# The value part of each chunk's right-hand side, computed in runs ahead of a chunked scan

## The chip, the cores and the metric

The kernel runs on one core of a Trainium2 chip. The metric is the device time of one execution, in microseconds (us). The kernel before took 1484.86, 1486.97 and 1489.13 us in three runs; the median is 1486.97.

## The reference

One step of a hybrid decoder layer, for 512 prompt tokens and 8 samples of 8 tokens (576 columns in all): a half-step SwiGLU network, three mixers side by side that are merged by gates (an RWKV-7 recurrence, a causal convolution, cross-attention into a memory), and a second half-step SwiGLU network. The change touches the recurrence alone. For each of eight heads it keeps a 64 x 64 state and goes token by token:

```python
def step(s, inp):
    r_t, w_t, k_t, v_t, kk_t, kka_t = inp
    sa = jnp.einsum('bhij,bhj->bhi', s, -kk_t)
    s = (s * w_t[:, :, None, :] + sa[..., None] * kka_t[:, :, None, :]
         + v_t[..., None] * k_t[:, :, None, :])
    return s, jnp.einsum('bhij,bhj->bhi', s, r_t)
```

The prompt starts from a zero state, each sample from its own. Outputs are the tokens' results and the states at the end.

## The kernel before

**The whole.** The first network, the mixers, the merge and the second network follow each other. All large products take their operands split into a high and a low part (helper `split`: a cast on ScalarE, L96, and a subtraction on VectorE, L97) and make three products of 128 x 128 weights with 288 columns (`mm3k`, L110). In the mixers such products are also the **filler** that runs beside the recurrence: projections, gates and the parts of the merge that are ready. A table, `PLAN`, writes down in which order the pieces are emitted; the framework's scheduler then interleaves them with a model of its own. Each engine works through its own queue strictly in the order that came out.

**The recurrence in chunks.** Two heads share the 128 partitions, so there are four head pairs j, each prepared (`prep`), partly inverted (`inverse`, on VectorE, then `joined`, two sets of sixteen 32 x 32 products, L987 and L995) and run by a **chain** (`chain`, L877). A chain has nine chunks of 64 tokens: eight of the prompt, one after the other, and a ninth (index 8) with the 64 tokens of the eight samples. `prep` makes, by L872 and a masking L874, the table `gr` of products inside each chunk.

The chain first transposes keys into `kbt` (L890) and values into rows 0 to 63 of `vu` (L894), four chunks to a PSUM bank, and copies them out on ScalarE (L895 for the values). Rows 64 to 127 of `vu` will hold the *solutions*, the vectors `sa` of each token in the chunk. They solve a triangular system; its right-hand side has a value part and a state part. Per prompt chunk c:

1. The value part: for each of the two heads a product of `gr` rows 0 to 63 with the values (L1003).
2. The state part: `ra` times the state before, added in the same PSUM bank (L1006).
3. ScalarE copies the sum to the tile `xs` (L1008); PE multiplies it by the inverse, head by head (L1010); ScalarE copies the solutions into `vu` (L1012).
4. `kbt` times the whole `vu` gives what the chunk adds to the state (L1021). ScalarE scales the old state (L1026) and VectorE forms the new one (L1030; L1033 in the first chunk), in a ring of three `st` tiles.
5. The outputs: L1036 for both heads and L1038 with the old state, copied out on ScalarE (L1039).

After the eight chunks follows `sample_chunk` (L1045): the same with eight states `ms` at once, so that L1006 and the outputs L1058 (eight columns each) are issued eight times; L1067 makes the additions to the states, L1070 and L1071 apply them on VectorE, and L1072 stores them. Then come centering (L904), sums (L138) and the gate (L128). The chain takes its PSUM banks from a pool of three (tag "c"); prep has two ("g"), the filler three ("p").

In the profile's names `st`, `xs`, `vu`, `kbt`, `gr`, `ra` and `ms` are the tiles above, `x`, `wh` and `wl` activations and split weights of the filler, `oc0h` and the like the split operands of merge products, `cst` the constants (identity among them), `lt`, `tt` and `pr` tiles of the inverse (its steps on VectorE are L965, L967 and L969), and `cc` the convolution's sum (L655, L656).

Of the kernel before, what the change touches and what calls it, by code (L numbers as in the profile page):

```python
# [6 lines left out]
F32 = mybir.dt.float32  # L7
F32R = mybir.dt.float32r
AF = mybir.ActivationFunctionType
ALU = mybir.AluOpType  # L10
# [6 lines left out]
NB = 8  # L17
# [33 lines left out]
class _Builder:  # L51
# [825 lines left out]
    def chain(self, j):  # L877
        V, A, T = self.V, self.A, self.T
        con, par = self.con, self.par
        ident = con("ident")  # L880
        b3 = self.b3
        gr, kb, v, ra, gc, bv = self.made[j]

        kbt = b3.tile([128, 9, 128], F32, name="kbt")
        vu = b3.tile([128, 9, 128], F32, name="vu")
        for c in range(0, 9, 4):
            n = min(4, 9 - c)
            ps = self.bank("c")
            for i in range(n):
                T.transpose(ps[:, i * 128:(i + 1) * 128], kb[:, c + i].rearrange("p a t -> p (a t)"), ident)  # L890
            A.copy(kbt[:, c:c + n, :], ps[:, :n * 128].rearrange("p (i t) -> p i t", t=128))
            ps = self.bank("c")
            for i in range(n):
                T.transpose(ps[:64, i * 128:(i + 1) * 128], v[:, (c + i) * 64:(c + i + 1) * 64], ident)  # L894
            A.copy(vu[:64, c:c + n, :], ps[:64, :n * 128].rearrange("p (i t) -> p i t", t=128))  # L895
        self.chunks(j, gr, kbt, vu, ra, gc)
        self.sample_chunk(j, gr, kbt, vu, ra, gc)


        sq, rs = (b3.tile([128, 640], F32, name="u2", bufs=2)[:, :N] for _ in range(2))  # L900
        for c0, c1 in ((0, 5), (5, 9)):
            c = slice(64 * c0, 64 * c1)
            p = self.bank("c")[:, :64 * (c1 - c0)]
# [91 lines left out]
                T.matmul(ps[64:96, h, c, :], zz[:, h, c, :32], gr[96:128, h, c, 96:128], start=True, stop=True)  # L995
        A.copy(gr[64:96, :, :8, 96:128], ps[64:96])

    def solve(self, c, gr, vu, inter):

        T = self.T  # L1000
        ps = self.bank("c")
        for h in range(2):
            T.matmul(ps[64:, 64 * h:64 * h + 64], gr[:64, h, c, 64:], vu[:64, c, 64 * h:64 * h + 64],  # L1003
                     start=h == 0 or not inter, stop=not inter)
        for i, (l, r) in enumerate(inter):
            T.matmul(ps[64:, :128], l, r, start=False, stop=i == len(inter) - 1)  # L1006
        xs = self.b3.tile([128, 128], F32, name="xs")
        self.A.copy(xs[64:], ps[64:, :128])  # L1008
        for h in range(2):
            T.matmul(ps[64:, 128 + 64 * h:192 + 64 * h], gr[64:, h, c, 64:], xs[64:, 64 * h:64 * h + 64],  # L1010
                     start=True, stop=True)
        self.A.copy(vu[64:, c, :], ps[64:, 128:256])  # L1012
        return ps

    def chunks(self, j, gr, kbt, vu, ra, gc):

        V, A, T = self.V, self.A, self.T
        m = None
        for c in range(8):
            ps = self.solve(c, gr, vu, [(ra[:, c, 1, :], m)] if c else [])  # L1020
            T.matmul(ps[:, 256:384], kbt[:, c, :], vu[:, c, :], start=True, stop=True)  # L1021
            self.st = self.st[1:] + self.st[:1]
            mn = self.st[0]
            if c:
                mg = self.b3.tile([128, 128], F32, name="mg", bufs=2)
                A.activation(mg, m, AF.Copy, scale=gc[:, c:c + 1])  # L1026
            for h in range(2):
                s = slice(64 * h, 64 * h + 64)
                if c:
                    V.scalar_tensor_tensor(mn[s, s], ps[s, 256 + 64 * h:320 + 64 * h], gc[s, c:c + 1], mg[s, s],  # L1030
                                           ALU.mult, ALU.add)
                else:
                    V.tensor_scalar(mn[s, s], ps[s, 256 + 64 * h:320 + 64 * h], gc[s, c:c + 1], None, ALU.mult)  # L1033
            for h in range(2):
                s = slice(64 * h, 64 * h + 64)
                T.matmul(ps[s, 384:448], vu[:, c, s], gr[:, h, c, :64], start=True, stop=c == 0)  # L1036
            if c:
                T.matmul(ps[:, 384:448], m, ra[:, c, 0, :], start=False, stop=True)  # L1038
            A.copy(ra[:, c, 0, :], ps[:, 384:448])  # L1039
            m = mn  # L1040
        for h in range(2):
            s = slice(64 * h, 64 * h + 64)
            self.store(self.a["wso"][j, s], m[s, s])

    def sample_chunk(self, j, gr, kbt, vu, ra, gc):  # L1045
        V, A, T = self.V, self.A, self.T
        b3 = self.b3
        ms, ax = self.ms, self.ax
# [5 lines left out]
        for h in range(2):  # L1054
            s = slice(64 * h, 64 * h + 64)
            T.matmul(ps[s, 384:448], vu[:, 8, s], gr[:, h, 8, :64], start=True, stop=False)
        for b in range(NB):
            T.matmul(ps[:, 384 + 8 * b:392 + 8 * b], ms[:, b, :], ra[:, 8, 0, 8 * b:8 * b + 8], start=False,  # L1058
                     stop=b == NB - 1)
        A.copy(ra[:, 8, 0, :], ps[:, 384:448])  # L1060
# [169 lines left out]
```

## Time and profile before

| | us |
|---|---|
| runs | 1484.86, 1486.97, 1489.13 |
| the profiled execution | 1487.49 |
| its span, first to last instruction | 1485.7 |
| PE (TensorE) busy | 1460.2 |
| weight loads busy (PEld) | 1378.1 |
| DVE (VectorE) busy | 1027.4 |
| ACT (ScalarE) busy | 675.5 |
| the four chains and what runs beside them | about 590 to 1000 |

The mean granted clock of TensorE was 0.982. In the rows, "c<-vu,gr" means that a tile of pool "c" was written from `vu` and `gr`; "64*64 64x64 ... x4" is the loaded weight, the columns streamed, and how many records the row holds. In a row of waits the three numbers are the sum in us, how many times, and the longest. Times in timelines count from the start of the span, and the second number is the duration. A number with "<-" in brackets is the engine's idle time just before, and what ended it.

### The profile page before, as it was taken

Reading aid. Unit: us, or ns where it says so; the run is one execution under the profiler, and the core shown is the slowest. Engines: PE = TensorE matmul, PEld = TensorE weight load, DVE = VectorE, ACT = ScalarE, POOL = GpSimd, SP = SyncE. Lnnn points to the kernel's source line nnn. Section 1 sums busy time; section 2 is a strip of 40 time slices with the busy share of each in tenths; the row PEclk is TensorE's granted clock in tenths of the full one; section 3 lists DMA queues with packets and bytes.
Section 4 is the critical chain, followed back from the end, with each engine's and each line's share of the span. In section 5 each row is a group of like instructions: output and inputs, shape, how many; then the busy total and the mean of one; then the engine's idle time right before and its main releaser. Section 6 shows DMA issues by size and latency. Waiting matters only on the chain.

```text
span 1485.7 us, 27013 instructions
## 1 busy us (share of the span) xinstructions
PE 1460.2 (98%) x10778; PEld 1378.1 (93%) x10778; DVE 1027.4 (69%) x2053; ACT 675.5 (45%) x1370; POOL 4.5 (0%) x21
## 2 busy tenths in 40 slices
PE   8999999999999999999999999999999999999997
PEld 8999999999998799888889888789999999999997
DVE  7976777777784579778466456357578767777775
ACT  6443344443577535435446542444354434444342
POOL 0000000000010000000000000000000000000000
PEclk9999999999999999999899999999999999999998
DMA  6222222232632243133123134255222322322221
GB/s 209 72 84 87 86 86 86 86 98 95 205 101 86 66 132 91 46 98 96 60 65 97 55 100 126 92 177 175 100 72 72 100 73 85 102 95 89 86 86 64
DMA packets 95033, 144.04 MB, mean 97 GB/s; under 512 B 43628, under 2 KB 53228, under 8 KB 94908
## 3 DMA queue, kind: packets, MB, share of 16 engines
q1 hardware_dynamic: 94332, 141.74, 30.9%
q8 instruction: 84, 1.38, 0.4%
q10 hardware_dynamic: 576, 0.59, 0.1%
q14 instruction: 41, 0.34, 0.1%
HBM read 126.07 MB, written 16.23 MB: 96 GB/s over the span
## 4 chain that ended last, share of the span: by engine, by line
PE 92%; DVE 4%; ACT 2%; DMA 1%; issue 1%; SPq 0%; DVEq 0%; ACTq 0%
PE p L110 51%; PE p L369 26%; PE g L872 1%; PE c L1006 1%; PE c L1010 1%; PE c L1003 1%; DVE pr L965 1%; PE g L128 1%; PE c L128 1%; PE c L1038 1%; PE c L1036 1%; DMA w<-win 1%; PE p L148 1%; PE c L1021 1%; PE c L1058 1%
## 5 line engine op out<-in xcount | busy, mean ns | idle before, releaser
L110 PE MATMUL p<-x,wh 128*128 128x288 f32 x3136 | 655.4, 300 | 1.1 <-ACT kv L541 0.7
L110 PEld LDWEIGHTS p<-x,wh 128*128 128x128 f32 x3136 | 507.1, 188 | 15.2 <-issue 7.9
L110 PE MATMUL p<-x,wl 128*128 128x288 f32 x1568 | 469.7, 300 | 1.5 <-DVE wl L97 1.5
L96 ACT CAST wh<-w 128x512 fp32r<-128x512 f32 (+1 forms) x353 | 209.5, 600 | 257.2 <-PE p L110 111.9
L97 DVE TENSOR_TENSOR wl<-w,wh 128x512 fp32r<-128x512 f32 (+1 forms) x353 | 231.9, 662 | 109.2 <-ACT wh L96 102.2
L110 PEld LDWEIGHTS p<-x,wl 128*128 128x128 f32 x1568 | 295.2, 188 | 7.0 <-issue 3.1
L369 PE MATMUL p<-t,wh 128*128 128x288 f32 x1088 | 224.2, 298 | 0.0
L369 PEld LDWEIGHTS p<-t,wh 128*128 128x128 f32 x1088 | 173.8, 188 | 6.4 <-DVE t L380 6.2
L369 PE MATMUL p<-b,wh 128*128 128x288 f32 x816 | 169.7, 295 | 0.0
L369 PE MATMUL p<-t,wl 128*128 128x288 f32 x544 | 160.5, 295 | 0.0
L96 ACT CAST wh<-p 128x512 fp32r<-128x512 f32 x136 | 84.5, 621 | 155.9 <-PE p L110 117.7
L369 PEld LDWEIGHTS p<-b,wh 128*128 128x128 f32 x816 | 132.6, 188 | 0.0
L97 DVE TENSOR_TENSOR wl<-p,wh 128x512 fp32r<-128x512 f32 x136 | 93.5, 688 | 50.4 <-ACT wh L96 47.8
L369 PE MATMUL p<-b,wl 128*128 128x288 f32 x408 | 120.3, 295 | 0.0
L369 PEld LDWEIGHTS p<-t,wl 128*128 128x128 f32 x544 | 102.4, 188 | 0.0
L369 PEld LDWEIGHTS p<-b,wl 128*128 128x128 f32 x408 | 76.8, 188 | 0.0
L446 DVE SCALAR_TENSOR_TENSOR x<-p,x 128x288 f32<-128x288 f32 x128 | 57.7, 451 | 20.3 <-PE p L110 20.3
L96 ACT CAST x<-t 128x576 fp32r<-128x576 f32 (+1 forms) x60 | 36.5, 610 | 45.6 <-DVE t L450 42.3
L1030 DVE SCALAR_TENSOR_TENSOR st<-c,gc,mg 64x64 f32<-64x64 f32 x56 | 15.9, 283 | 53.3 <-PE c L1021 52.5
L359 DVE TENSOR_TENSOR p<-w 128x512 f32<-128x512 f32 x68 | 46.7, 686 | 3.2 <-DMA w<-wu 2.7
L359 DVE TENSOR_TENSOR p<-p,w 128x512 f32<-128x512 f32 x68 | 46.3, 681 | 0.1
L110 PE MATMUL p<-x,t 128*128 128x288 f32 x264 | 38.5, 306 | 5.5 <-ACT t L96 5.5
(345 smaller groups left out, 1987.8 us busy)
## 6 DMA issues: line engine op xcount, KB each, us to landing
w<-wu SPq DMA_DIRECT2D x85, 512.0 KB
w<-win SPq DMA_DIRECT2D x44, 512.0 KB
w<-wd SPq DMA_DIRECT2D x64, 256.0 KB
w<-wd SPq DMA_DIRECT2D x16, 384.0 KB
d_mb<-gate SPq DMA_DIRECT2D x16, 288.0 KB
w<-wo SPq DMA_DIRECT2D x8, 512.0 KB
x<-x SPq DMA_DIRECT2D x8, 288.0 KB
d_x<-x SPq DMA_DIRECT2D x16, 144.0 KB
```

The source lines that it names most:

```text
L96: self.A.copy(hi, x)
L97: self.V.tensor_tensor(lo, x, hi.bitcast(F32), ALU.subtract)
L110: self.T.matmul(p, l, x[r][:, c], start=k == 0 and i == 0, stop=k == n - 1 and i == 2)
L128: self.T.matmul(p, l, r[:, c], start=i == 0, stop=i == len(ops) - 1)
L148: self.T.matmul(p[:, o + f - d.start:o + 128 - d.start], r[f:, i], self.con("ident")[f:, f:], start=True, stop=True)
L359: V.tensor_tensor(s, u, v, ALU.add)
L369: self.T.matmul(p, hl[l][:, c], xs[k][b][:, o], start=first and k == 0 and q == 0, stop=k == 3 and q == 2, skip_group_check=True)
L446: V.scalar_tensor_tensor(x[m][:, c], p, 0.5, x[m][:, c], ALU.mult, ALU.add)
L872: T.matmul(ps[:, i * 128:(i + 1) * 128], kb[o, c + i].rearrange("p a t -> p (a t)"), ra[o, c + i].rearrange("p a t -> p (a t)"), start=Tru ...
L965: V.tensor_tensor(pr, tt[:, :n, :e].unsqueeze(2).broadcast_to([np_, n, m, e]), l3[:, t:e, :e].unsqueeze(1).broadcast_to([np_, n, m, e]), A ...
L1003: T.matmul(ps[64:, 64 * h:64 * h + 64], gr[:64, h, c, 64:], vu[:64, c, 64 * h:64 * h + 64], start=h == 0 or not inter, stop=not inter)
L1030: V.scalar_tensor_tensor(mn[s, s], ps[s, 256 + 64 * h:320 + 64 * h], gc[s, c:c + 1], mg[s, s], ALU.mult, ALU.add)
```

## The change

The values of all nine chunks are transposed first. The value parts of the right-hand sides are then computed in runs over four chunks and both heads: eight products into one PSUM bank, a second eight, and two for the ninth chunk. ScalarE copies each run into the rows of `vu` that will later hold the solutions. Between the runs stand the transposes of the keys. In a chunk the state product now fills a bank alone; VectorE adds it to what lies in `vu`, in place; the inverse is applied from there, and the solutions overwrite it. The tile `xs` is gone. Chunk 0 has no state part and takes the rows as they are.

The samples' chunk is cut in four pieces. Right-hand side: ahead of chunk 0. Solution: after chunk 0's. Outputs: ahead of chunk 1. The states: after chunk 1's solution.

```diff
         vu = b3.tile([128, 9, 128], F32, name="vu")
-        for c in range(0, 9, 4):
-            n = min(4, 9 - c)
+        groups = [(c, min(4, 9 - c)) for c in range(0, 9, 4)]
+        by = lambda ps, n: ps[:, :n * 128].rearrange("p (i t) -> p i t", t=128)
+        for c, n in groups:
+            ps = self.bank("c")
+            for i in range(n):
+                T.transpose(ps[:64, i * 128:(i + 1) * 128], v[:, (c + i) * 64:(c + i + 1) * 64], ident)
+            A.copy(vu[:64, c:c + n, :], by(ps[:64], n))
+        for c, n in groups:
+
+            ps = self.bank("c")
+            for i in range(n):
+                for h in range(2):
+                    o = slice(64 * h, 64 * h + 64)
+                    T.matmul(by(ps[64:], n)[:, i, o], gr[:64, h, c + i, 64:], vu[:64, c + i, o], start=True, stop=True)
+            A.copy(vu[64:, c:c + n, :], by(ps[64:], n))
             ps = self.bank("c")
             for i in range(n):
                 T.transpose(ps[:, i * 128:(i + 1) * 128], kb[:, c + i].rearrange("p a t -> p (a t)"), ident)
...
-        self.chunks(j, gr, kbt, vu, ra, gc)
-        self.sample_chunk(j, gr, kbt, vu, ra, gc)
+        sample = self.sample_chunk(j, gr, kbt, vu, ra, gc)
+        self.chunks(j, gr, kbt, vu, ra, gc, lambda: next(sample, None))
...
-    def solve(self, c, gr, vu, inter):
-
-        T = self.T
-        ps = self.bank("c")
+    def solve(self, c, gr, vu, ps):
+
         for h in range(2):
-            T.matmul(ps[64:, 64 * h:64 * h + 64], gr[:64, h, c, 64:], vu[:64, c, 64 * h:64 * h + 64],
-                     start=h == 0 or not inter, stop=not inter)
-        for i, (l, r) in enumerate(inter):
-            T.matmul(ps[64:, :128], l, r, start=False, stop=i == len(inter) - 1)
-        xs = self.b3.tile([128, 128], F32, name="xs")
-        self.A.copy(xs[64:], ps[64:, :128])
+            self.T.matmul(ps[64:, 128 + 64 * h:192 + 64 * h], gr[64:, h, c, 64:], vu[64:, c, 64 * h:64 * h + 64],
+                          start=True, stop=True)
+        self.A.copy(vu[64:, c, :], ps[64:, 128:256])
...
         for c in range(8):
-            ps = self.solve(c, gr, vu, [(ra[:, c, 1, :], m)] if c else [])
+            if c < 2:
+                beside()
+            ps = self.bank("c")
+            if c:
+                T.matmul(ps[64:, :128], ra[:, c, 1, :], m, start=True, stop=True)
+                V.tensor_tensor(vu[64:, c, :], ps[64:, :128], vu[64:, c, :], ALU.add)
+            self.solve(c, gr, vu, ps)
+            if c < 2:
+                beside()
             T.matmul(ps[:, 256:384], kbt[:, c, :], vu[:, c, :], start=True, stop=True)
...
-        ps = self.solve(8, gr, vu, [(ax[:, b, :], ms[:, b, :]) for b in range(NB)])
...
+        ps = self.bank("c")
         for b in range(NB):
...
+            T.matmul(ps[64:, :128], ax[:, b, :], ms[:, b, :], start=b == 0, stop=b == NB - 1)
+        V.tensor_tensor(vu[64:, 8, :], ps[64:, :128], vu[64:, 8, :], ALU.add)
+        yield
+        self.solve(8, gr, vu, ps)
+        yield
+        self.outputs(8, gr, vu, ra, ps, [(slice(8 * b, 8 * b + 8), ms[:, b, :]) for b in range(NB)])
+        yield
```

`outputs` is a new function with the products of step 5 and their copy. New line numbers: value transposes L891, runs L899 and their copy L900, key transposes L903, inverse applied L1010, outputs L1018 and L1020, state product L1033, the add L1034, addition to the state L1038, new state L1047 and L1050, samples' right-hand side L1068, their states L1079, L1081, L1084 and L1085, centering L913; join L996 and L1004.

The order of instructions shows the move at three places. A chunk step of the second chain on PE, before:

```order
L1036 MATMUL c<-gr,vu 64x64 x2
L1038 MATMUL c<-ra,st_5290 128x64
L1006 MATMUL c<-st_5291,ra 64x128
L110 MATMUL p<-x_4933,wh 128x288
L110 MATMUL p<-x_4932,wl 128x288
L110 MATMUL p<-x_4934,wh 128x288
L1003 MATMUL c<-vu,gr 64x64 x2
L110 MATMUL p<-x_4935,wh 128x288
L1010 MATMUL c<-xs,gr 64x64 x2
```

and with the change:

```order
L1018 MATMUL c<-gr,vu 64x64 x2
L1020 MATMUL c<-ra,st_5291 128x64
L1033 MATMUL c<-st_5289,ra 64x128
L110 MATMUL p<-x_4930,wl 128x288
L110 MATMUL p<-x_4932,wh 128x288
L110 MATMUL p<-x_4933,wh 128x288
L110 MATMUL p<-x_4932,wl 128x288
L1010 MATMUL c<-vu,gr 64x64 x2
```

The value product of the next chunk, L1003, no longer stands alone between two fillers; the four fillers between the state product and the inverse now follow each other. Second, the start of the last chain on PE, before:

```order
L987 MATMUL c<-aux,gr 32x32 x16
L995 MATMUL c<-gr,aux 32x32 x16
L890 MATMUL c<-cst,kb 128x128 x4
L894 MATMUL c<-cst,v 64x128 x4
L890 MATMUL c<-cst,kb 128x128 x4
L894 MATMUL c<-cst,v 64x128 x4
L890 MATMUL c<-cst,kb 128x128
L110 MATMUL p<-cb0h,wh 128x288
L110 MATMUL p<-cb0l,wh 128x288
L894 MATMUL c<-cst,v 64x128
```

and with the change:

```order
L996 MATMUL c<-aux,gr 32x32 x16
L1004 MATMUL c<-gr,aux 32x32 x16
L891 MATMUL c<-cst,v 64x128 x9
L899 MATMUL c<-vu,gr 64x64 x8
L110 MATMUL p<-cb0h,wh 128x288
L110 MATMUL p<-cb0l,wh 128x288
L110 MATMUL p<-cb0h,wl 128x288
L110 MATMUL p<-cb1h,wh 128x288
L110 MATMUL p<-cb1l,wh 128x288
L903 MATMUL c<-cst,kb 128x128 x4
L899 MATMUL c<-vu,gr 64x64 x8
L903 MATMUL c<-cst,kb 128x128 x4
```

All value transposes come first, the first run of eight follows them with nothing between, and the second stands between transposes of keys. Third, DVE in the first chunks of the second chain, with the change:

```order
L1047 SCALAR_TENSOR_TENSOR st_5290<-c,gc,mg 64x64 x2
L783 TENSOR_TENSOR gate<-p,gate 128x288 x2
L1034 TENSOR_TENSOR vu<-c,vu 64x128
L97 TENSOR_TENSOR wl<-w,wh 128x512
L963 MEMSET lt 108x32
L966 MEMSET lt 108x11
L97 TENSOR_TENSOR wl<-w,wh 128x256
L1047 SCALAR_TENSOR_TENSOR st_5291<-c,gc,mg 64x64 x2
```

The add L1034 is new in this queue; ahead of it stand two gate operations (L783), behind it a split of weights (L97).

More of the change, by code (lines that the diff above doesn't have):

```diff
@@ L890, in chain @@
                 T.transpose(ps[:, i * 128:(i + 1) * 128], kb[:, c + i].rearrange("p a t -> p (a t)"), ident)
-            A.copy(kbt[:, c:c + n, :], ps[:, :n * 128].rearrange("p (i t) -> p i t", t=128))
-            ps = self.bank("c")
-            for i in range(n):
-                T.transpose(ps[:64, i * 128:(i + 1) * 128], v[:, (c + i) * 64:(c + i + 1) * 64], ident)
-            A.copy(vu[:64, c:c + n, :], ps[:64, :n * 128].rearrange("p (i t) -> p i t", t=128))
-        self.chunks(j, gr, kbt, vu, ra, gc)
-        self.sample_chunk(j, gr, kbt, vu, ra, gc)
+            A.copy(kbt[:, c:c + n, :], by(ps, n))
+        sample = self.sample_chunk(j, gr, kbt, vu, ra, gc)
+        self.chunks(j, gr, kbt, vu, ra, gc, lambda: next(sample, None))
         sq, rs = (b3.tile([128, 640], F32, name="u2", bufs=2)[:, :N] for _ in range(2))
@@ L996, in joined, with outputs, chunks @@
         A.copy(gr[64:96, :, :8, 96:128], ps[64:96])
-    def solve(self, c, gr, vu, inter):
-        T = self.T
-        ps = self.bank("c")
+    def solve(self, c, gr, vu, ps):
         for h in range(2):
-            T.matmul(ps[64:, 64 * h:64 * h + 64], gr[:64, h, c, 64:], vu[:64, c, 64 * h:64 * h + 64],
-                     start=h == 0 or not inter, stop=not inter)
-        for i, (l, r) in enumerate(inter):
-            T.matmul(ps[64:, :128], l, r, start=False, stop=i == len(inter) - 1)
-        xs = self.b3.tile([128, 128], F32, name="xs")
-        self.A.copy(xs[64:], ps[64:, :128])
-        for h in range(2):
[L1010 to L1015, printed above, removed]
+            self.T.matmul(ps[64:, 128 + 64 * h:192 + 64 * h], gr[64:, h, c, 64:], vu[64:, c, 64 * h:64 * h + 64],
+                          start=True, stop=True)
+        self.A.copy(vu[64:, c, :], ps[64:, 128:256])
+    def outputs(self, c, gr, vu, ra, ps, states):
+        for h in range(2):
+            s = slice(64 * h, 64 * h + 64)
+            self.T.matmul(ps[s, 384:448], vu[:, c, s], gr[:, h, c, :64], start=True, stop=not states)
+        for i, (t, m) in enumerate(states):
+            self.T.matmul(ps[:, 384 + t.start:384 + t.stop], m, ra[:, c, 0, t], start=False, stop=i == len(states) - 1)
+        self.A.copy(ra[:, c, 0, :], ps[:, 384:448])
+    def chunks(self, j, gr, kbt, vu, ra, gc, beside):
         V, A, T = self.V, self.A, self.T
@@ L1033, in chunks @@
                     V.tensor_scalar(mn[s, s], ps[s, 256 + 64 * h:320 + 64 * h], gc[s, c:c + 1], None, ALU.mult)
[L1034 to L1039, printed above, removed]
+            self.outputs(c, gr, vu, ra, ps, [(slice(0, 64), m)] if c else [])
             m = mn
@@ L1052, in sample_chunk @@
         A.copy(_q8(ax.rearrange("p b t -> p (b t)"), 72)[:, :, :8], _q8(ra[:, 8, 1, :], 8))
-        ps = self.solve(8, gr, vu, [(ax[:, b, :], ms[:, b, :]) for b in range(NB)])
-        for h in range(2):
-            s = slice(64 * h, 64 * h + 64)
-            T.matmul(ps[s, 384:448], vu[:, 8, s], gr[:, h, 8, :64], start=True, stop=False)
+        ps = self.bank("c")
         for b in range(NB):
-            T.matmul(ps[:, 384 + 8 * b:392 + 8 * b], ms[:, b, :], ra[:, 8, 0, 8 * b:8 * b + 8], start=False,
-                     stop=b == NB - 1)
-        A.copy(ra[:, 8, 0, :], ps[:, 384:448])
+            T.matmul(ps[64:, :128], ax[:, b, :], ms[:, b, :], start=b == 0, stop=b == NB - 1)
[5 more added lines that the diff above has]
+        yield
         ps = self.bank("c").rearrange("p (b v) -> p b v", v=64)
```

## The prediction

> **What bounds the kernel now.** I read the busy table first, then the chain of waits, then the waits of the one engine that they name.
>
> ```profile
> PE 1460.2 (98%) x10778; PEld 1378.1 (93%) x10778; DVE 1027.4 (69%) x2053; ACT 675.5 (45%) x1370; POOL 4.5 (0%) x21
> PE 92%; DVE 4%; ACT 2%; DMA 1%; issue 1%; SPq 0%; DVEq 0%; ACTq 0%
> ...
> PE c L987 <- DMA aux<-s: 2.0, 1, 2.0
> PE p L110 <- DVE wl L97: 1.3, 2, 1.1
> ...
> PE c L1036 <- DVE st L1030: 0.4, 1, 0.4
> ```
>
> TensorE is busy 98% of the span and is 92% of the chain of waits. The last three rows are its waits in 590 to 1000 us, the stretch of the four chains: the longest is 2.0 us, and all of them together come to about 8 us of 410. Nothing that PE waits for can pay much there; what PE itself does between two products can. So I looked at the rate at which PE's stream goes on. One chunk step of chain 0, seen in the weight loads (start, duration, line, x passes; every product here is two or more passes, each with its own load):
>
> ```profile
> 627.22 0.19 PEld L1006 LDWEIGHTS c<-st,ra 128*64 128x64 f32 x2
> 627.58 0.19 PEld L110 LDWEIGHTS p<-x,wl 128*128 128x128 f32 x1 [0.17 <-issue]
> 627.69 0.33 PEld L110 LDWEIGHTS p<-x,wh 128*128 128x128 f32 x2
> 628.18 0.30 PEld L1003 LDWEIGHTS c<-vu,gr 64*64 64x64 f32 x4 [0.16 <-ACT xs L1008]
> 628.56 0.19 PEld L110 LDWEIGHTS p<-x,wl 128*128 128x128 f32 x1
> 628.88 0.30 PEld L1010 LDWEIGHTS c<-xs,gr 64*64 64x64 f32 x4
> 629.26 0.19 PEld L110 LDWEIGHTS p<-oc0h,wh 128*128 128x128 f32 x1
> 629.37 0.19 PEld L110 LDWEIGHTS p<-oc0l,wh 128*128 128x128 f32 x1
> 629.50 0.19 PEld L110 LDWEIGHTS p<-oc0h,wl 128*128 128x128 f32 x1
> 629.64 0.19 PEld L110 LDWEIGHTS p<-oc1h,wh 128*128 128x128 f32 x1
> ...
> 630.03 0.32 PEld L1021 LDWEIGHTS c<-vu,kbt 128*128 128x128 f32 x2
> 630.27 0.19 PEld L110 LDWEIGHTS p<-oc0h,wh 128*128 128x128 f32 x1
> ```
>
> The L110 products (the filler) follow each other every 0.13 us (629.37, 629.50, 629.64). From 627.83, where the second load of the 627.69 pair starts (its end less 0.19), to 629.26 are 1.43 us. Two filler products of 0.13 lie in it and two trips away from the filler, L1003 and L1010. So a trip costs (1.43 − 0.26) / 2 = **0.58 us**. The work in it is small: four passes last 0.30 us, one alone 0.133 (the group row below), so a further pass adds (0.30 − 0.133) / 3 = 0.056, four 0.22. The other **0.36 us** is the change of form, there and back.
>
> **The change, part by part.** *Value products in runs.* The same 36 pairs (9 chunks, 4 chains) are computed, in 12 runs of eight, eight and two products, next to the transposes that open the chain. Their passes are only moved. What falls away are trips: the order of PE's instructions over the four chains has 165 departures from the L110 stream before and 138 after, 27 fewer, 24 of them L1003 alone between two fillers, as at 628.18. The number of L110 products is the same. Saving: 27 × 0.36 = **−9.7 us**. From below, a trip that stays in the filler's own form, L1021, takes 0.24 (630.03 to 630.27), 0.13 beyond two passes of 0.056, so −3.5; from above, the whole 0.58 gives −15.7. I take 0.36, since L1003 is the very instruction that goes.
> The Trainium skill ("TensorE: Matmul & The Clock Gate", Part 2, on LDWEIGHTS in the step-by-step) speaks against a price: weight loads are pulled ahead of the products in flight where the row groups don't conflict or the background buffer takes them. By it a trip costs its passes alone, nothing is saved, and the sum ends 2.4 us above before, at 1489.4. The trace agrees where the form stays (L110's loads of 0.19 at a pace of 0.13) and not where it changes (0.36).
>
> *Copy replaced by an add.* ACT's copy to xs goes; the state product is added by DVE to what lies in vu. Rows of the groups, one of ACT's timeline, and the windows of the four chains (stretch, us, busy PE, PEld, DVE, ACT, POOL, then granted clock, DMA share, GB/s):
>
> ```profile
> L1003 PEld LDWEIGHTS c<-vu,gr 64*64 64x64 f32 x144 | 10.8, 133 | 5.2 <-ACT xs L1008 2.9 <-issue 1.0 <-ACT ra L1039 0.2
> ...
> L1008 ACT COPY xs<-c 64x128 f32<-64x128 f32 x36 | 9.4, 261 | 7.6 <-PE c L1006 4.7 <-PE c L1003 2.5
> L895 ACT COPY vu<-c 64x512 f32<-64x512 f32 x8 | 4.6, 580 | 1.7 <-PE c L894 1.7
> ...
> L874 DVE TENSOR_TENSOR gr<-g,cst 128x128 f32<-128x128 f32 x6 | 1.7, 288 | 3.3 <-PE g L872 3.2
> L1030 DVE SCALAR_TENSOR_TENSOR st<-c,gc,mg 64x64 f32<-64x64 f32 x56 | 15.9, 283 | 53.3 <-PE c L1021 52.5
> L655 DVE SCALAR_TENSOR_TENSOR cc<-up,pv,cc 128x512 f32<-128x512 f32 x38 | 27.7, 746 | 0.1
> ...
> 627.75 0.26 ACT L1008 COPY xs<-c 64x128 f32<-64x128 f32 x1 [0.21 <-PE c L1006]
> ...
> 601.00:648.00 47.00, 47.00 (x347) 37.39 (x348) 28.29 (x64) 15.42 (x47) 0.00 (x0) 0.97 0.22 70
> 713.00:768.00 55.00, 55.00 (x431) 45.18 (x431) 20.72 (x65) 19.97 (x57) 0.00 (x0) 0.91 0.19 57
> 835.00:882.00 47.00, 46.59 (x348) 36.86 (x346) 19.06 (x56) 17.58 (x53) 0.00 (x0) 0.98 0.25 75
> 923.00:975.00 52.00, 50.37 (x379) 39.88 (x380) 17.12 (x37) 20.61 (x59) 0.00 (x0) 0.88 0.27 82
> ```
>
> The nearest to the add is L874, the same operation from PSUM, 0.288 us, against 0.261 for the copy. The copy starts 0.53 after the state product (627.75 − 627.22), so L1010 could go 0.53 + 0.29 + about 0.05 = 0.87 after it. Between the two now stand three or four fillers and L1003's trip (1.66 us, 627.22 to 628.88); in the change mostly four to six fillers, by the rows above 0.36 + 0.11 + 3 × 0.13 + 0.35 = about 1.2 us for four. The cover shrinks from 0.8 to 0.3 us. DVE may stand in an operation of 0.75 us (L655) as the product ends; with DVE busy 42% of the windows (85.2 of 201 us) and 0 to 0.75 us of it left, what passes 0.3 is 0.45² / 2 / 0.75 × 0.42 = 0.06 us a step on average. For 28 steps that is 1.7, less in the 16 with five fillers or other PE work between: **+1.3 us**. From below 0 (the 53.3 us that DVE idles ahead of L1030 say that it is mostly free); from above a whole L655 ahead of each add, 28 × (0.75 − 0.3) = +12.6. Behind the waiting add stand splits of weights (L97), for which PE waits 1.3 us in all as it is, and the inverse's steps. ACT, freed of 9.4 us and given 12 copies like L895 (5.7 at most), is no bound.
>
> *Chain starts.* In the last chain nine transposes and the first run stand together without filler, so the run waits for its copy: **+0.6** (L895). One chunk step there has no filler at all between its state product and L1010: 0.87 − 0.36 = **+0.5**.
>
> *Samples' chunk beside chunks 0 and 1.* Its passes are the same, and its state loads and stores are moved on SP's queue: one store now stands ahead of two of the loads that open inverse 1. Its DVE work moves from the end to the start of the chain. These rows tell what that can reach:
>
> ```profile
> 703.54 0.30 SPq L978 DMA_DIRECT2D aux<-s  x1
> ...
> 713.08 1.08 PEld L987 LDWEIGHTS c<-aux,gr 32*32 32x32 f32 x32 [0.39 <-issue]
> ...
> 923.05 1.19 PE L987 MATMUL c<-aux,gr 32*32 32x32 f32 x32 [2.01 <-DMA aux<-s]
> ...
> 911.64 0.51 DVE L967 TENSOR_REDUCE tt<-pr 108x11 f32<-108x352 f32 x1
> ```
>
> Inverse 1's last load is issued 9.5 us before PE reads it, so a few us at its start are covered. Inverse 3 is the one waited for: its last DVE step ends at 912.15, and 10.9 us of transfers follow. DVE is relieved just before that, and PE arrives earlier by what it saved: between +2 and −2, taken as **0**.
>
> *The granted clock.*
>
> ```profile
> 641.46:644.87 3.41, 3.41 (x32) 3.11 (x32) 1.81 (x4) 0.62 (x2) 0.00 (x0) 1.00 0.05 10
> 644.87:648.28 3.41, 3.41 (x10) 1.33 (x9) 0.68 (x1) 0.21 (x1) 0.00 (x0) 0.50 0.00 0
> 713.14:716.55 3.41, 3.41 (x74) 3.21 (x74) 1.54 (x6) 0.86 (x4) 0.00 (x0) 1.00 0.17 44
> 716.55:726.79 10.24, 10.24 (x50) 9.05 (x50) 2.56 (x5) 3.22 (x7) 0.00 (x0) 0.50 0.09 15
> ...
> 641.67 1.86 PEld L1058 LDWEIGHTS c<-ra,ms 128*128 128x128 f32 x16
> ...
> 723.58 0.87 PEld L890 LDWEIGHTS c<-cst,kb 128*128 128x128 f32 x4
> ```
>
> Stretches of 3.41 us stand at 0.50. They follow 3.41 us full of products of few columns: at 641.46 the sixteen passes of eight columns for the samples' outputs, at 713.14 the join's 32x32. A pass costs 0.116 us at 641.67 and 0.218 at 723.58, so such a stretch costs 1.7 us. Over the four chains (length × twice what the clock lacks: 2.8 + 9.9 + 1.9 + 12.5) 27 us stand at half, 8 stretches, 13.5 us of loss. The change takes the narrow outputs away from the chain's end and puts transposes and products of half the rows at its start, in two or three stretches each. I take **0** net, ±3.
>
> Sum: −9.7 + 1.3 + 0.6 + 0.5 = **−7.3 us**. The profiled run took 1487.49 (span 1485.7 and 1.8 around it), so 1480.2 in its terms; the median shown, 1486.97, lies 0.5 below it: **1479.7 us**, 0.5% less. Its own range, with the clock's ±3 and ±2.6 for a trip's price 0.1 to either side, is 1479.7 ± 4 (root of the squares): 1475.7 to 1483.7.
>
> **Rivals.** *The steps wait for the add.* The place is DVE's queue at the add, where a split or an L655 stands ahead. At 0.2 to 0.3 us in each of the 28 steps 6 to 8 us come back, in place of 1.3: net −1 to −3, **1485**. For it: the cover shrinks to 0.3 us, and 0.75 us operations are there. Against it: the state updates depend on DVE in the same way now, and PE waits 0.4 us for them in all. A price of a trip near the lower bound, or none at all, ends within 0.3% too and is counted here.
>
> *The ends run at full clock.* Without the narrow outputs the stretch after 641.46 and its like at the other chains' ends are not halved: three of the 8 are 5 us more, **1474.5**. For it: the row at 644.87. Against it: the centering and sums that follow are thin too, and the passes come back beside chunks 0 and 1.
>
> *The starts run at half clock, and it is slower.* Nine transposes and eight products of 64 rows in one block could take a whole 3.41 us in which PE counts as idle, as the join does at 713.14, in each chain, for two stretches more. The gain of 7.3 is gone at 4 added stretches, and slower by over 0.3% it is from 7 on; 8 make +13.6 − 7.3 = +6.3, **1493**. For it: the 10.24 us at 0.50 in just this place. Against it: the half-clock time of all chains would have to double, while the transposes are there already and each run is only 16 × 0.056 = 0.9 us.
> The Trainium skill speaks for this rival (same page, Part 4): transposes do not count as busy for the gate in the same way. By it the sum would be this rival's 1493. At 716.55 the trace agrees so far, though half-row products stand there with them.
>
> *The change doesn't do what it says*: the order shows 27 trips fewer, so only their price can fail, which the first rival holds.
>
> **How the numbers follow.** Forecast 0.54, the add's waits 0.22, full clock at the ends 0.15, half clock at the starts 0.09. No change means within 0.3%, 4.5 us, about what a measurement of this kernel can tell: 1482.5 to 1491.4. Faster: nearly all of the 0.54, 0.15 and a little of the first rival, 0.70; slower: most of the last, 0.08; the rest 0.22. The range runs from the full-clock case to past the add's waits: 1474 to 1486.5, which leaves out the last rival and the tails.
>
> **What will show it.** Right: no L110 gap at the old place of L1003, runs of 16 loads at a pace near 0.056, and PE's busy time in the middle down by 8 to 10 us with its waits up by at most 3. Wrong in the add: rows "PE c L1010 <- DVE vu L1034" of over 5 us. Wrong in the trips: fillers at each chunk's start still paying 0.36 where L1003 stood. Wrong in the clock: the four chains' granted clock, weighted as above, off 27 us at half by more than 7.

## The result: slower, by 1.1%

The changed kernel took 1501.24 us (median of six runs, 1497.56 to 1509.24) against 1484.94 for the kernel before (six runs, 1484.25 to 1489.13). The ratio is 1.0112, with a 95% interval of 1.0088 to 1.0135. The forecast was 1479.7, in a range of 1474 to 1486.5, with a chance of 0.08 for slower. In one later kernel (`e3_out_end`) a run of 1505.6 us counts as slow and is left out of the ratio, though not of the median.

The page of the changed kernel (profiled execution 1499.2 us) and its clock:

```profile
PE 1468.3 (98%) x10778; PEld 1384.8 (92%) x10778; DVE 1037.3 (69%) x2085; ACT 674.8 (45%) x1348; POOL 4.6 (0%) x21
PE 90%; DVE 5%; ACT 2%; DMA 1%; issue 1%; SPq 0%; DVEq 0%; ACTq 0%
...
core 0: 1497.4 us, clock 0.974
```

TensorE is still the engine that is busy, now for 8 us longer, with the same number of instructions. The clock is the first thing that has moved: 0.974 for 0.982. The waits of PE in 590 to 1010 us:

```profile
PE g L138 <- ACT u L834: 1.6, 1, 1.6
PE p L110 <- ACT wh L96: 1.5, 3, 1.0
PE c L1038 <- ACT vu L1012: 1.5, 1, 1.5
PE c L996 <- DMA aux<-s: 1.4, 1, 1.4
...
PE c L1018 <- DVE st L1047: 0.7, 1, 0.7
...
PE c L1010 <- DVE vu L1034: 0.4, 1, 0.4
```

All waits there come to 10.8 us, for 7.2 before. The wait for the new add, in the last row, is 0.4 us in all (the weight loads ahead of L1010 stood still for it four times, 2.3 us together): the rival that I feared most is not there. 3.6 us of waits do not make 16.

The windows do. For each of three places, the 3.41 us before a halving of the clock and the stretch at half that follows (columns as in the prediction):

```profile
611.92:615.33 3.41, 3.41 (x31) 2.97 (x29) 1.69 (x4) 1.96 (x3) 0.00 (x0) 1.00 0.15 43
615.33:618.75 3.42, 3.42 (x17) 2.81 (x17) 0.93 (x3) 0.33 (x2) 0.00 (x0) 0.50 0.00 0
618.75:622.16 3.41, 3.41 (x13) 1.45 (x11) 1.38 (x3) 1.28 (x3) 0.00 (x0) 0.50 0.03 5
622.16:625.57 3.41, 3.41 (x15) 3.09 (x14) 2.82 (x5) 0.00 (x0) 0.00 (x0) 0.50 0.00 0
642.63:646.05 3.42, 1.57 (x8) 0.80 (x6) 2.79 (x11) 3.34 (x6) 0.00 (x0) 1.00 0.63 162
646.05:652.87 6.82, 6.82 (x30) 5.58 (x30) 5.15 (x12) 3.79 (x9) 0.00 (x0) 0.50 0.29 88
...
966.86:970.28 3.42, 2.34 (x17) 1.58 (x16) 2.70 (x6) 1.41 (x5) 0.00 (x0) 1.00 0.16 61
970.28:980.52 10.24, 10.24 (x45) 8.15 (x43) 2.61 (x8) 2.47 (x8) 0.00 (x0) 0.50 0.33 101
```

And two of the instructions in them, from PE's timeline:

```profile
613.78 2.21 PE L1020 MATMUL c<-ra,ms 128*128 128x8 f32 x16
...
968.15 0.34 PE L1018 MATMUL c<-gr,vu 128*64 128x64 f32 x4 [0.68 <-DVE st L1047]
```

At 612 us it is the samples' outputs, sixteen passes of eight columns, now beside the chain's first chunks. At 643 it is the wait of 1.5 us for L1012, at 967 the chunk step without filler, with 0.68 us of waiting. Between 590 and 1010 us the changed kernel has 18 stretches of 3.41 us at half, the kernel before 11. Six of the 18 follow the samples' outputs directly (four before), four stand at the chains' starts (five before), and eight follow waits and thin steps elsewhere (two before). Seven more, at half of 3.41 us each, are 11.9 us, and the two spans lie 11.7 apart. That the two agree so closely is in part luck: PE's saved trips and its longer waits lie in the same spans, and at the 0.43 us per us found next the seven come to 10.3.

The same holds from run to run. The half-clock time of a run is 2 × (1 − its mean clock) × its span. The six runs of the change went from 1497.56 us at a clock of 0.975 (75 us at half) to 1509.24 at 0.966 (102 us): 11.7 us for 27.7, or 0.42 us of time per us at half. A line through all six has the slope 0.43 and leaves 0.5 us. So I give for every kernel below its median, its median half-clock time, and the **rest**, the mean of time less 0.43 × half-clock time; in no kernel is its standard deviation above 1.3 us.

### The profile page after: what moved, and what is told of

The parts are those of the page before. It is cut to its first block, busy times and chain, and to the rows that moved or that the text cites. A ratio compares the mean times of both kernels' runs of the same rounds, so it can differ in the third digit from the quotient of the medians.

```text
span 1497.4 us, 27035 instructions
## 1 busy us (share of the span) xinstructions
PE 1468.3 (98%) x10778; PEld 1384.8 (92%) x10778; DVE 1037.3 (69%) x2085; ACT 674.8 (45%) x1348; POOL 4.6 (0%) x21
## 4 chain that ended last, share of the span: by engine, by line
PE 90%; DVE 5%; ACT 2%; DMA 1%; issue 1%; SPq 0%; DVEq 0%; ACTq 0%
PE p L110 50%; PE p L369 26%; DVE pr L974 1%; PE c L1020 1%; PE g L872 1%; PE c L1010 1%; PE c L899 1%; DVE tt L976 1%; PE c L1033 1%; PE g L128 1%; PE c L1018 1%; PE c L1081 1%; DVE wl L97 1%; DMA w<-win 1%; PE p L148 1%
## 5 line engine op out<-in xcount | busy, mean ns | idle before, releaser
L110 PEld LDWEIGHTS p<-x,wh 128*128 128x128 f32 x3136 | 512.4, 191 | 15.8 <-issue 8.9
L96 ACT CAST wh<-w 128x512 fp32r<-128x512 f32 (+1 forms) x353 | 209.6, 600 | 265.6 <-PE p L110 116.3
L97 DVE TENSOR_TENSOR wl<-w,wh 128x512 fp32r<-128x512 f32 (+1 forms) x353 | 231.9, 662 | 110.8 <-ACT wh L96 103.1
L110 PEld LDWEIGHTS p<-x,wl 128*128 128x128 f32 x1568 | 298.3, 191 | 6.1 <-issue 3.3
L96 ACT CAST wh<-p 128x512 fp32r<-128x512 f32 x136 | 84.4, 621 | 155.7 <-PE p L110 117.3
L97 DVE TENSOR_TENSOR wl<-p,wh 128x512 fp32r<-128x512 f32 x136 | 93.7, 689 | 50.5 <-ACT wh L96 47.7
L96 ACT CAST x<-t 128x576 fp32r<-128x576 f32 (+1 forms) x60 | 36.5, 610 | 45.7 <-DVE t L450 42.4
L655 DVE SCALAR_TENSOR_TENSOR cc<-up,pv,cc 128x512 f32<-128x512 f32 x60 | 44.1, 747 | 0.2
```

What stands on the lines that cost most here:

```text
L96: self.A.copy(hi, x)
L97: self.V.tensor_tensor(lo, x, hi.bitcast(F32), ALU.subtract)
L110: self.T.matmul(p, l, x[r][:, c], start=k == 0 and i == 0, stop=k == n - 1 and i == 2)
L655: V.scalar_tensor_tensor(c[:, :SEQ], up[:, k:k + SEQ], w, c[:, :SEQ], ALU.mult, ALU.add)
```

## Experiments: the two halves of the change, and the place of the samples' chunk

Three theories stood at first: A, the samples' chunk beside the first chunks; B, the runs at the chain's start; C, the add. Four kernels were held against each other.

**The runs alone** (`e1_runs`). The samples' chunk goes back behind the eight chunks.

```diff
-        self.chunks(j, gr, kbt, vu, ra, gc, lambda: next(sample, None))
+        self.chunks(j, gr, kbt, vu, ra, gc, lambda: None)
+        for _ in sample:
+            pass
```

> The runs of value products and the add alone; the samples' chunk stays whole behind the eight chunks, as before. Theory A (the samples' thin products beside the first chunks pull the clock down and stand in the way of the chunk steps): with them back at the end the half-clock time of the middle falls from about 61 us to about 40, the 27 saved trips show, and the time is 1478 to 1484. Theory B (the runs and all transposes at the start of each chain are what loses the clock): it stays at 1494 to 1502, with about 60 us at half clock, at the starts. Theory C (the add makes every chunk step wait): 1488 to 1494, with the half-clock time of before and more us of PE in the chunk steps.

Measured: 1492.7 us (twelve runs, 1481.6 to 1503.0), ratio 1.0045 [1.0016, 1.0073]; 69 us at half (44 to 93), for 46 of the kernel before in the same comparison (26 runs, 1485.5 us). The rest is 1463.4, against 1464.9 before. Theory A is not enough: half the loss, and 23 of the 36 us at half clock, are here without it. By its time alone the kernel lies in C's range, but C falls: nothing in the trace waited for the add L1034 (L1036 in this kernel), and the half-clock time is not that of before. B has the half-clock time, but its place only in part: three of the entries still follow the samples' outputs at the chains' ends, as before; nine stretches stand at the starts, for five. The rest is only 1.5 us lower, where the saved trips should have taken off some 8; where that went is not shown.

**The samples' chunk alone** (`e2_beside`). Value products, copy and inverse per chunk as before.

```diff
-        self.chunks(j, gr, kbt, vu, ra, gc)
-        self.sample_chunk(j, gr, kbt, vu, ra, gc)
+        sample = self.sample_chunk(j, gr, kbt, vu, ra, gc)
+        self.chunks(j, gr, kbt, vu, ra, gc, lambda: next(sample, None))
...
         for c in range(8):
-            ps = self.solve(c, gr, vu, [(ra[:, c, 1, :], m)] if c else [])
+            if c < 2:
+                beside()
+            ps, xs = self.rhs(c, gr, vu, [(ra[:, c, 1, :], m)] if c else [])
+            self.solve(c, gr, vu, ps, xs)
+            if c < 2:
+                beside()
```

> The samples' chunk beside the first two chunks alone; value products, copy and inverse per chunk as before (the samples' own copy goes to its rows of vu in place of xs). Theory A: about as slow as the changed kernel less what the trips save, 1497 to 1505, with 55 us or more at half clock in the middle, also inside the chains. Theory B: 1483 to 1488, half-clock time as before, about 37 us. Theory C: as B.

Measured: 1492.3 us, ratio 1.0052 [1.0035, 1.0068]; 55 us at half, rest 1468.7. That lies between the ranges of A (1497 to 1505) and B (1483 to 1488) and is a miss for both. One half of the loss comes by the clock (9 us more, some 4 us of time), the other by a rest that is 3.8 us higher. I had priced the move of the samples' chunk at nothing.

**Only the first two pieces beside chunk 0** (`e3_out_end`).

```diff
-            if c < 2:
+            if c < 1:
                 beside()
```

(at both places, and the remaining pieces behind the chunks as in the first kernel)

> The changed kernel with only the first two pieces of the samples' chunk (right-hand side, solution) beside chunk 0; the outputs (sixteen passes of eight columns) and the states go back behind the eight chunks. If within theory A the outputs and states are what starts the half clock: close to the run with all of the samples' chunk behind the chunks, 1479 to 1486. If the right-hand side's sixteen passes do it: 1492 to 1502. Theory B: 1494 to 1502.

Measured: 1487.9 us (twelve runs, 1480.5 to 1505.6), ratio 1.0019 [0.9999, 1.0039]; 58 us at half, rest 1463.2. Outputs and states taken out of the chunk steps give back 13 of the 16 us. The right-hand sides of the samples, whose sixteen passes stream 128 columns each, seem not to be the trouble; with runs 25 us apart it is no closer than that.

**The pieces beside chunks 3 and 4** (`e4_mid`).

```diff
-            if c < 2:
+            if 3 <= c < 5:
                 beside()
```

> The changed kernel with the same four pieces beside chunks 3 and 4 in place of 0 and 1. If in theory A it is the meeting of the samples' thin products with the chain's start (transposes, runs, joins) that loses the clock: half-clock time falls and the time is 1480 to 1490. If thin products among the chunk steps lose it wherever they stand: 1496 to 1504, with the half-clock stretches in the chains' middle. Theory B: 1494 to 1502, with the stretches still at the starts.

Measured: 1496.5 us, ratio 1.0082 [1.0056, 1.0109]; 81 us at half, rest 1461.9. As in the last sentence but one of what was expected: among the chunk steps they lose the clock in both places tried.

## Experiments: the width of the samples' outputs

Counting the moving columns of the products in each stretch of 3.41 us gave a rule that none of the theories had. A first count put its border at about 2500 columns, which is theory D below; the numbers here are from thirteen profiles, of the kernels below too, all but that of `e3_out_end`. Of 73 stretches at full clock with fewer than 2600 columns, 61 were followed by half clock; of 2266 with more, 30. Of the stretches at half, 76 of the 99 with fewer stayed at half, and 10 of the 77 with more. With transposes left out of the count, the wrong calls at full clock rise from 42 to 64. The share of a stretch in which the profile has PE busy does worse: at its best border, half of the stretch, it calls 18 of the 91 entries and misses 73. (The count is a fit to these traces; the trace shows no such counter, and the numbers move by some ten with the way in which a product across an edge is counted.) A filler product streams 288 columns in 0.13 us. Sixteen passes of eight columns stream 128 in 1.9.

This can be tried without leaving work out: the tile `ax` holds the samples' vectors in a block diagonal, and once the right-hand sides have read it, it can hold `r` instead. Each pass of the outputs then streams 64 columns, zeros outside its eight, for one more copy on ScalarE per chain. `f_after` is the changed kernel with this edit alone, `f_before` the kernel before with it; `f_e1`, `f_e4` and `f_e2` have it on top of the kernels above.

```diff
-            self.T.matmul(ps[:, 384 + t.start:384 + t.stop], m, ra[:, c, 0, t], start=False, stop=i == len(states) - 1)
+            self.T.matmul(ps[:, 384:448], m, t, start=False, stop=i == len(states) - 1)
...
-        self.outputs(8, gr, vu, ra, ps, [(slice(8 * b, 8 * b + 8), ms[:, b, :]) for b in range(NB)])
+        A.copy(_q8(ax.rearrange("p b t -> p (b t)"), 72)[:, :, :8], _q8(ra[:, 8, 0, :], 8))
+        self.outputs(8, gr, vu, ra, ps, [(ax[:, b, :], ms[:, b, :]) for b in range(NB)])
```

> The changed kernel, with the samples' outputs streamed 64 columns wide in place of 8: r is copied into the block diagonal of ax once the right-hand sides have read it, and each of the sixteen passes streams all 64 columns of its block, zeros outside. Same weights, same number of passes, same results. Theory D (the clock is halved by a stretch of 3.41 us in which few columns are streamed, under about 2500, whatever the instructions are, and the sixteen passes of 8 columns make such a stretch in each chain): the entries at 612, 854 and 946 us go, with the two or three stretches that follow each, half-clock time falls from 82 us to 55 to 65 and the time from 1501 to 1488 to 1493, although nothing is left out. Theory E (PE counts as idle by waits, or transposes and small weights lose the clock): the same passes of the same small stationary work keep 75 us or more at half and 1498 to 1504.

Measured: 1491.0 us, ratio 1.0035 [1.0021, 1.0049]; 51 us at half for 82: the time is in theory D's range, the half-clock time 4 us below it. The group of the samples' outputs in 590 to 1010 us, first in the changed kernel, then with wide outputs, and last the windows at the same place in the chain with wide outputs:

```profile
L1020 PE MATMUL c<-ra,ms 128*128 128x8 f32 x64 | 8.4, 265 | 0.0
```

```profile
L1020 PE MATMUL c<-ax,ms 128*128 128x64 f32 x64 | 8.6, 280 | 0.0
```

```profile
611.00:614.41 3.41, 3.41 (x32) 2.91 (x30) 2.38 (x5) 2.02 (x4) 0.00 (x0) 1.00 0.16 43
614.41:617.83 3.42, 3.42 (x23) 2.14 (x19) 1.71 (x3) 0.86 (x4) 0.00 (x0) 1.00 0.00 0
```

Eight times the columns cost PE 0.2 us more in 64 passes, and the clock stays at 1.00 behind them. 32 us at half clock are gone, nearly as many as the 36 that the change had added; how many of these belong to the new place of the outputs, the next kernel tells. The time fell by 10.2, where 0.43 × 32 would be 13.7; the rest rose by 3.7 (waits for weight splits among it: 6.5 us for L96 and L97 together, 2.3 in the changed kernel).

> The kernel before, with the samples' outputs 64 columns wide in the same way. Theory D: the stretches that begin after the samples' outputs at the chains' ends (641, 877, 966 us; one or two each) go, half-clock time from 46 to about 30 to 36 us, time 1479 to 1482. Theory E: 1485 to 1487 and the half-clock time of before.

Measured: 1479.6 us, ratio 0.9960 [0.9946, 0.9973]; 30 us at half for 46, and the entries at the chains' ends are gone. The same edit makes the kernel before faster.

It takes 16 us at half from the kernel before, where it took 32 from the changed one. So by this difference the outputs' new place accounts for about 16 of the 36 us. With wide outputs on both sides the change still adds 21 us at half (51 for 30) and 11.4 us of time, 9 of them by the clock. In the profiles most of these stand at the starts of the second and the fourth chain, first with the change, ten stretches, then without it, three:

```profile
713.44:733.92 20.48, 20.48 (x114) 17.49 (x111) 3.25 (x6) 6.45 (x12) 0.00 (x0) 0.50 0.12 30
925.07:938.72 13.65, 13.65 (x98) 11.96 (x99) 1.38 (x2) 5.53 (x11) 0.00 (x0) 0.50 0.24 86
```

```profile
718.08:724.90 6.82, 6.71 (x31) 5.59 (x31) 1.97 (x5) 1.83 (x4) 0.00 (x0) 0.50 0.13 22
919.46:922.88 3.42, 3.42 (x23) 3.10 (x21) 0.69 (x1) 2.46 (x5) 0.00 (x0) 0.50 0.42 134
```

What narrow outputs do is clear over all five pairs of kernels (before, the change, runs alone, samples' chunk alone, beside chunks 3 and 4): in their profiles 17 of the 20 groups of narrow outputs are followed directly by half clock, and none of the 20 groups of wide ones.

> The runs of value products and the add, the samples' chunk behind the chunks, its outputs 64 columns wide. Theory D: the entries after the samples' outputs (759, 879, 971 us) go, half-clock time from 69 to about 45 to 52 us; by 1463.4 + 0.43 x half-clock time that is 1483 to 1486. Theory E: 1491 to 1494.

Measured: 1500.0 us, ratio 1.0076 [1.0048, 1.0105], 72 us at half. A miss. The entries after the samples' outputs are gone here too, but the chains' starts took their place:

```profile
716.33:733.40 17.07, 17.07 (x90) 14.30 (x90) 1.53 (x4) 6.13 (x12) 0.00 (x0) 0.50 0.11 27
815.32:828.97 13.65, 13.65 (x96) 12.39 (x94) 1.99 (x3) 5.88 (x11) 0.00 (x0) 0.50 0.23 83
938.20:955.26 17.06, 17.06 (x105) 14.97 (x103) 2.38 (x5) 7.24 (x16) 0.00 (x0) 0.50 0.19 55
```

Fourteen stretches in three blocks, where the kernel before has five (716.55 to 726.79, and two at 925) and its wide form three. This is the mechanism of my slower rival, as far as the profile shows it. The join's products of 32 columns, or a wait at the join, halve the clock (which of the two was not tried); value transposes, value products and key transposes then stand in one block, and at half clock such a block streams mostly 1600 to 2600 columns in 3.41 us, too few to win it back.

> The changed kernel with the samples' pieces beside chunks 3 and 4, and the outputs 64 columns wide. Theory D: half-clock time from 81 to 50 to 60 us; by 1461.9 + 0.43 x half-clock time 1483 to 1488. Theory E: 1494 to 1499.

Measured: 1477.8 us, ratio 0.9946 [0.9929, 0.9964]; 38 us at half for 81, rest 1460.9. That is 5 us below theory D's range. It is the fastest kernel of the study, faster than both kernels of the comparison; but of the 7.8 us below the kernel before, `f_before` has 6.0 by the wide outputs alone, and the 1.7 between these two are within what the intervals leave open. Its second and fourth chain open with the same products as `f_e1`'s, and no stretch there is at half: by the count above, the second chain's opening streams 3072 to 3808 columns per stretch at full clock (709.8 to 720.1). So the block kept the full clock here and the half clock there; it looks as if the join ahead of it decides, which was not tried by itself.

> The samples' chunk beside the first two chunks with the solution per chunk as before, and the samples' outputs 64 columns wide. It asks what the move of the samples' chunk costs once its outputs no longer halve the clock; to be held against 1479.6 us (wide outputs, samples' chunk at the end, 30 us at half). Theory H (the move costs 3 to 5 us of its own, in waits and in more trips away from the filler; with narrow outputs the time less 0.43 of the half-clock time was 3.8 above before): 1482 to 1486 with 28 to 36 us at half. Theory I (without the clock the move is free): 1478 to 1481.

Measured: 1489.2 us, ratio 1.0017 [1.0003, 1.0031]; 37 us at half. It is 9.6 us slower than `f_before`, of which the clock explains 0.43 × 7.6 = 3.3. That is theory H, at more than its price. The waits of this kernel in 590 to 1010 us:

```profile
PE p L110 <- ACT wh L96: 3.6, 2, 3.4
PE p L110 <- DVE wl L97: 3.4, 3, 1.8
PE c L987 <- DMA aux<-s: 3.1, 1, 3.1
PE p L110 <- DVE gate L783: 1.4, 3, 0.6
```

They come to 14.4 us in all (with five smaller rows), 8.0 in `f_before`. The longest is a filler product waiting for a cast, which on ScalarE stands behind two table loads of 1.28 us: with the samples' chunk moved, the scheduler orders the filler and the splits differently. That the waits come from that order was seen in this profile only and not tried by itself.

## Experiments: the chain's opening cut in two

The transposes and value products of chunks 4 to 7 (in the second and third kernel also of the ninth) are emitted ahead of chunk 2 instead of at the start. All three have wide outputs.

```diff
+        def opening(groups):
...
+        opening(groups[::2])
...
         for c in range(8):
+            if c == 2:
+                rest()
```

> The changed kernel with the samples' outputs 64 columns wide, and the chain's opening cut in two: transposes and value products of chunks 4 to 7 are emitted ahead of chunk 2 in place of the chain's start. Theory F (join, transposes, value products of half the rows and key transposes in one block stream under 2500 columns in 3.41 us once the clock is half, so a halving at the join lasts until fillers come; four to six stretches in the wide-output run of the changed kernel): the streaks at the starts of the second and fourth chain fall to two or three, half-clock time from 51 to 35 to 40 us, time from 1491 to 1483 to 1487. Theory G (the streaks follow from the join alone, or from where the free-running window happens to lie): the half-clock time stays at 48 to 55 us and the time within 3 us of 1491.

Measured: 1482.3 us, ratio 0.9979 [0.9962, 0.9996]. The time is a little better than theory F had it, the reason is not F's: 47 us at half for 51, and the streaks at the two starts are four stretches each, after six and four. The rest fell by 6.6 us, to 1462.4, with waits of 8.8 us for 12.5.

> The runs and the add with the samples' chunk at the end, outputs 64 columns wide, and the opening of chunks 4 to 8 ahead of chunk 2. Without the cut this kernel took 1500 us, with five stretches at the start of the second chain, three at the third and five at the fourth. Theory F: half-clock time from 72 to 35 to 45 us and the time to 1481 to 1488. Theory G: 1494 to 1501.

Measured: 1480.6 us, ratio 0.9965 [0.9952, 0.9978]; 47 us at half for 72. Here F holds in kind, 2 us above its range at half clock:

```profile
715.22:725.46 10.24, 10.15 (x52) 8.75 (x51) 2.07 (x5) 3.44 (x5) 0.00 (x0) 0.50 0.09 16
...
920.00:933.66 13.66, 12.74 (x111) 11.34 (x107) 2.92 (x7) 5.77 (x13) 0.00 (x0) 0.50 0.10 37
```

Three and four stretches for five and five; at the third chain what is left, two stretches at 814, lies ahead of its transposes. The 25 us less at half are worth 10.6 of the 19.4 us; the others are a rest 8.1 us lower, for which F has no reason.

> The kernel with the samples' pieces beside chunks 3 and 4, outputs 64 columns wide, and the opening of chunks 4 to 8 ahead of chunk 2. Without the cut 1477.8 us, with 38 us at half and short streaks at the starts. Theory F: 30 to 36 us at half, 1473 to 1477. Theory G: 1476 to 1480.

Measured: 1484.6 us, ratio 0.9986 [0.9967, 1.0005]; 50 us at half (29 to 69) for 38. A miss for both theories: it lost what it was to gain.

All kernels together (us; the kernel before is measured anew beside each group, 1484.9 to 1486.9):

| kernel | median | at half clock | rest |
|---|---|---|---|
| before (26 runs) | 1485.5 | 46 | 1464.9 |
| the change | 1501.2 | 82 | 1465.3 |
| runs alone | 1492.7 | 69 | 1463.4 |
| samples' chunk alone | 1492.3 | 55 | 1468.7 |
| two pieces beside chunk 0 | 1487.9 | 58 | 1463.2 |
| pieces beside chunks 3, 4 | 1496.5 | 81 | 1461.9 |
| before, wide | 1479.6 | 30 | 1468.0 |
| the change, wide | 1491.0 | 51 | 1469.0 |
| runs alone, wide | 1500.0 | 72 | 1468.3 |
| samples' chunk alone, wide | 1489.2 | 37 | 1473.0 |
| beside chunks 3, 4, wide | 1477.8 | 38 | 1460.9 |
| the change, wide, cut | 1482.3 | 47 | 1462.4 |
| runs alone, wide, cut | 1480.6 | 47 | 1460.2 |
| beside chunks 3, 4, wide, cut | 1484.6 | 50 | 1463.5 |

## Why the prediction was wrong

**The bound and the trips: right in kind, a little too large.** Summing from one product's start to the next over 1600 filler products in both profiles, with those at half counted at the full-clock mean, the fillers went from 246.3 to 240.9 us and the value products from 12.8 to 10.1. That is 8.1 us of PE's pace, where 9.7 was predicted. The price of 0.36 for a change of form was a mean of L1003's and L1010's trips; over the whole trace the L1003 trips added 0.46 us each to the filler's pace and the L1010 trips 0.55.

**The add: right in size.** PE waited 0.4 us at L1010, its weight loads 2.3, for a predicted 1.8 with the step without filler; in the runs alone nothing waited for it. That step was predicted at 0.5 us, and its weight load waited 0.63 at just that place (969.59 in the last chain).

**The granted clock: the step that failed.** I wrote "The change takes the narrow outputs away from the chain's end and puts transposes and products of half the rows at its start, in two or three stretches each. I take 0 net, ±3." In its place the runs showed 36 us more at half clock, which is 15.7 of the 16.3 us lost (0.43 × 36.5; at the 0.35 of the kernel before alone it would be 12.8). Three things were missing in the step. It followed the narrow outputs away from the end, but not to where they went: into the steps of the first chunks, where they cost 32 us at half for 16 at the ends, as the wide outputs show (a rival named the place, without a price). It took the starts to be no worse than before, where the change adds 21 us with wide outputs on both sides. And it counted a halving at 3.41 us. At the chain's end, where dense filler follows, that is what it lasts at 645 and 880 before (two stretches at 969). Inside a chain it lasts until a stretch of enough columns comes: 10.24 us at 615 and 10.24 at 970. By the same reading a wait is dearer than its length: the three waits and thin steps ahead of 646, 820 and 970 us were 1.1 to 2.1 us each, and seven stretches at half follow them. (The prediction's 27 us at half left out or cut short the stretches at and beyond the edges of its four windows; the profile has 11 between 590 and 1010 us, not 8. Its price of 1.7 us for a stretch was reached by setting a pass of 8 columns beside a transpose, two different products; 0.43 of 3.41 us is 1.5.)

**The other terms together: −7.3 predicted, none of it seen.** The rest of the changed kernel is 0.4 us above before. This is the second thing that failed, and its cause is known only in part: the waits, 3.6 us longer, and the samples' chunk.

**The samples' chunk at 0: wrong.** By itself, beside the first two chunks, it costs 3.8 and 5.0 us of rest (1468.7 against 1464.9; 1473.0 against 1468.0 with wide outputs). It is no fixed price: with the runs it is 1.9 and 0.7 (the change against the runs alone), and beside chunks 3 and 4 the rest is lower than with the chunk at the end. I had looked at its queue entries and at the join, not at how the filler would be ordered around it. The wait at the join, priced at ±2, did little: 1.4 us for 2.0.

**The rivals.** The waits for the add did not come. "The ends run at full clock" was half true: the entries after the samples' outputs left the ends, but waits and the step without filler put others there. The slower rival named the right mechanism, and its price (8 more stretches, 1493) was close to the profile's 7; its time was 10 us short, since the 7.3 us that it set against them did not show. It looked for the cause at the starts, which in the one profile of the changed kernel have four stretches, for five before. With wide outputs its own cause showed: ten stretches there with the change, 14 with the runs alone, three in the kernel before. So it was right about roughly half of the loss. It deserved far more than 0.09: the rows quoted for the clock showed 13.5 us of loss in the four chains, and the change moved the very instructions beside them.

The Trainium skill's rule that was weighed for that rival ("TensorE: Matmul & The Clock Gate", Part 4: transposes do not count as busy) does not fit these traces: a count with the transposes in it sorts the stretches better than one without, 42 wrong calls for 64. The Trainium skill's rule that spoke against a price for trips (same page, Part 2) is not borne out either: 8.1 us of PE's pace were saved.

**What stays open.** The rest of the changed kernel is no lower than before, though 8.1 us of PE's pace were saved. The waits account for 3.6; the samples' chunk costs about 4 in its own kernel, partly in such waits, but in the runs alone, without it, the rest is only 1.5 us lower. A rest 7.0 and 7.7 us below `f_before`, about what the trips should bring, showed in two kernels, `f_e4` and `g_e1`. Whether the slope of 0.43 holds down to no half clock in every kernel is not known either: the 26 runs of the kernel before have 0.35 by themselves, which would put its rest 3.5 us higher; single kernels have slopes from 0.29 to 0.59, so differences of a few us between their rests are not certain. And why the cut opening helped two kernels and hurt the third was not settled; kernels that do the same work in another order differ by 10 us at half and more (72 in `f_e1`, 38 in `f_e4`).

## What to carry to other kernels

Where the granted clock falls in stretches, ask of each instruction that moves how many columns per microsecond it streams, and what stands behind it in its new place: here a thin stretch cost one or two stretches at half at the chains' ends and up to six ahead of more thin work. Where a pass takes as long with 8 columns as with 64, it can stream more of them, zeros too, and this was worth more here (0.4% on the kernel before) than the removal of 27 trips. When the time of a kernel scatters by more than half a per cent from run to run, plot it against the clock before comparing medians.

## What was not expected of the hardware

Sixteen passes of 64 columns took 2.15 us and of 8 columns 2.1 (8.6 and 8.4 us in 64 passes), with 128 x 128 weights in float32. Time against half-clock time is a straight line in every kernel, with a scatter of no more than 1.3 us (standard deviation) around it and 0.43 us per us at half in the changed one. The same kernel ran with 44 and with 93 us at half on the same chip (1481.6 and 1503.0 us, the runs alone): the instructions are the same. That the 3.41 us stretches fall on other instructions from run to run would explain it, but one run of each kernel was traced, so this is not shown.
